# A recurrence with three chain banks on both diagonals of TensorE, and a triangular inverse in blocks of 16 that TensorE joins to blocks of 32

## The chip, the cores and the metric

The kernel runs on one core of one Trainium2 chip. Its time is the device time of one execution in microseconds (us). Three runs of the kernel before took 1589.51, 1591.01 and 1592.47 us; the median is 1591.01 us. The engines are named PE (TensorE's matmuls), PEld (its weight loads), DVE (VectorE), ACT (ScalarE), POOL (GpSimd) and SP (the engine that issues most DMAs).

## The reference

Two blocks over 512 tokens of width 1024 and 256 context tokens. The change lies in the first block's mixer, in its recurrent half: 8 heads of width 64, two directions, 768 steps each.

```
def wkv_scan(state0, r, decay, kk, b, v, k, reverse):
    def step(S, inp):
        r_t, w_t, kk_t, b_t, v_t, k_t = inp
        sa = jnp.einsum("bhvk,bhk->bhv", S, kk_t)
        S = (S * w_t[:, :, None, :] - sa[..., None] * b_t[:, :, None, :]
             + v_t[..., None] * k_t[:, :, None, :])
        return S, jnp.einsum("bhvk,bhk->bhv", S, r_t)
    ...
for d in range(N_DIR):
    decay = exp(-DECAY_SCALE * sigmoid(w0[d] + tanh(w_lo) @ w_up[d]))
    a = sigmoid(a0[d] + a_lo @ a_up[d])
    k_d = k * (1 + (a - 1) * k_a)
    state, y = wkv_scan(init[d], rh, to_heads(decay), kk, kk * to_heads(a), vh, to_heads(k_d),
                        reverse=(d == 1))
    y_sum = y if y_sum is None else y_sum + y
```

After it come a group norm and a gate of y, the projection `w_out`, a conv FFN, and the second block (gated recurrence, windowed attention, conv FFN). All of it is float32.

## The kernel before, in words

**The stages.** `proj` computes the first block's projections and, among them, the preparation of head pair 0. `rwkv` then runs four `stage(j)`, one for each pair of heads. A pair's two heads lie in the partitions 0–63 and 64–127, so one product of 64x64 is two matmuls (`mmh`, L633), one on each of two diagonal quadrants of the 128x128 array; in the trace each of them leaves two records. `tail` holds the rest, from `out_proj1` (L885) on.

**The chain.** The 768 tokens are 12 chunks of 64. A stage makes 12 steps g, each for both directions d: 48 steps in all. For a chunk, `pr` = AS·V + KR·S0 is copied to R (ACT, L757), `pu` = XT·R is copied to U (L759), `p3` = kbt·V + id·S0 + kbt·U becomes the next state S0 (L769), and `py` = AS·V + KR·S0 + AS·U becomes Y (L188). All four outputs of a direction lie in one PSUM bank (`c10`, `c11`), and a token (`order="c1{d}"`) keeps a bank's matmuls in the order in which the code writes them. AS is the masked product of `psc`, put in place by DVE (L731); `kbt` is evacuated by ACT.

**The inverse.** XT holds, for each chunk and direction, the inverse of a unit triangle of 64. `inverse` (L650) takes AK (from `prep`), transposes 32x32 blocks into U (L663), makes 31 row steps on DVE, each a multiplication (L671) and a subtraction (L672), transposes X to F1 and F2 (L674, L675), and joins blocks of 32 to 64 by TensorE with 32x32 matmuls (`pt` L691, `po` L698 and L699). Each pass over PSUM goes by halves `D` of 12 blocks; ACT evacuates them.

**The order.** A scheduler issues by priority. Each chain step hands out some units of `todo`, a chain of generators: `prep(j+1)` (low-rank products, decay, KB, KR, AK, then its `inverse`), after the last one `splits`, `ada12` and `first`. `ada12` loads 32 pieces of 512 KB on SP's queue and DVE reduces each (L538, L539); `first` splits `wout` for the first two output tiles of `out_proj1` (`ahead`), which `rwkv` multiplies after the chain. `ada12` starts once `prep(3)` is done and its pool is closed. Then `gn` of the last stage (L781) gives the last operand `ahi7`, and `px` is completed.

Of the kernel before, what the change touches and what calls it, by code (L numbers as in the profile page):

```python
# [18 lines left out]
P = 128  # L19
# [20 lines left out]
for _n, _w in (("ident", 128), ("ones", 128), ("blk", 128), ("hind", 2), ("m0", 192), ("m1", 192), ("id2", 64), ("bsel", 6), ("hsel", 128), ("scan", 780)):  # L40
    CST[_n] = (_off, _w)
    _off += _w
# [3 lines left out]
def lay(I):  # L46
# [30 lines left out]
    for n, (s, w) in VEC.items():  # L77
# [21 lines left out]
         "bsel": np.kron(np.eye(64, 6), np.ones((2, 1))), "hsel": np.concatenate([np.tile(np.kron(np.eye(2), np.ones((1, 64))), (6, 1)), np.zeros((116, P))], 0)}  # L99
    c["id2"] = np.concatenate([np.eye(64)] * 2, 0)  # L100
# [22 lines left out]
class K:  # L123
# [120 lines left out]
    def build(self):  # L244
        tc = self.tc
        with ExitStack() as es:
# [10 lines left out]
            with ExitStack() as er:  # L257
                r0 = self.r0 = self.pool(er, "r0", side="left")
                self.sg = r0.tile([P, NX], F32, name="sg")
                self.vD = self.dr.tile([P, 4, 12, 64], F32, name="vD")  # L260
                self.rD, self.kD, self.kkD = [[self.dr.tile([P, n], F32, name=f"{t}D{j}") for j in range(4)] for t, n in (("r", NX), ("k", NT), ("kk", NT))]
                st = lambda p, name, shape: p.tile([P] + shape, F32, name=name)
                XT0, XT1 = self.XT0, _ = st(r0, "XT0", [24, 64]), zxb[:, 5:8, :].rearrange("p a (b c) -> p (a b) c", c=64)
                set0 = {"KB": [st(r0, f"KB0{d}", [12, 2, 64]) for d in range(2)], "KR": [st(r0, f"KR0{d}", [1280]) for d in range(2)]}
                self.sets = [dict(set0, XT=XT0), {"XT": XT1}, None, dict(set0, XT=XT0)]
                self.hb, self.kah = st(r0, "hb", [16]), st(r0, "kah", [4, 4])
                with ExitStack() as ep:
                    self.pp = self.pool(ep, "pp", side="right")
# [8 lines left out]
                    self.AK = st(self.pp, "AK", [32, 64])  # L277
# [21 lines left out]
    def proj(self):  # L299
# [62 lines left out]
        nc.gpsimd.memset(self.AK, 0.0)  # L362

# [23 lines left out]
        def k_post(j, px, pc):  # L387
# [4 lines left out]
            kr = self.pp.tile([P, 1024], F32, tag="inv", name="kr", bufs=3)[:, 0:NT]  # L392
# [85 lines left out]
    def rwkv(self, es, ep):  # L478
# [5 lines left out]
        self.C1 = [self.ps2.tile([P, 512], F32, name=f"c1{d}") for d in range(2)]  # L484
        for t in (*self.AS[0], *self.AS[1]):
            nc.vector.memset(t, 0.0)
        todo, gn = self.todo, iter(())
        for j in range(4):
# [3 lines left out]
            if j == 1:  # L492
# [4 lines left out]
                self.mmbufs, self.axbufs, self.wbufs, self.wsbufs = 6, 2, 3, 4  # L497
# [46 lines left out]
    def prep(self, j):  # L544
# [26 lines left out]
        for d in range(2):  # L571
# [51 lines left out]
            for q in range(2):  # L623
                pa = psm(384, "pa")
                for c in range(6 * q, 6 * q + 6):
                    kp = krc[:, c, :] if c < 4 else krx[:, c - 4, 0, :]
                    lt, rt_ = (kp, kb[:, c, bs, :]) if d else (kb[:, c, bs, :], kp)
                    self.mmh(pa[:, (c - 6 * q) * 64:(c - 6 * q) * 64 + 64], lt, rt_)
# [21 lines left out]
    def inverse(self, j):  # L650
# [4 lines left out]
        big = lambda name: pp.tile([P, 32, 32], F32, tag="inv", name=name, bufs=3)  # L655
# [6 lines left out]
        U, tmp, X = big("U"), big("tmp").rearrange("p a b -> p (a b)"), big("X")  # L662
        nc.vector.transpose(out=U, in_=AK[:, :, 0:32].rearrange("p n i -> p i n"))  # L663
        nc.gpsimd.memset(X, 0.0)
        nc.gpsimd.memset(X.rearrange("p a b -> p (a b)")[:, ::33], 1.0)
        for k in range(31):
            if k % 4 == 0:
                yield
            n, w = 31 - k, k + 1
            tv = tmp[:, 0:n * w].rearrange("p (a b) -> p a b", b=w)  # L670
            nc.vector.tensor_tensor(out=tv, in0=U[:, k + 1:32, k:k + 1].to_broadcast([P, n, w]), in1=X[:, k:k + 1, 0:w].to_broadcast([P, n, w]), op=ALU.mult)  # L671
            nc.vector.tensor_tensor(out=X[:, k + 1:32, 0:w], in0=X[:, k + 1:32, 0:w], in1=tv, op=ALU.subtract)  # L672
# [4 lines left out]
        D = slice(0, 12), slice(12, 24)  # L677
        for r, F in zip(D, (F1, F2)):
# [5 lines left out]
        T = big("T")  # L684
        ps = lambda name: self.psp.tile([P, 12, 32], F32, tag="inv", name=name, bufs=1)
# [18 lines left out]
    def stage(self, j, S, todo, rb, gn):  # L704
# [35 lines left out]
        for g in range(12):  # L740
            at = base + self.PK * g
            with self.prio(at):
# [3 lines left out]
                for d in range(2):  # L746
# [7 lines left out]
                    mm(pr, A[:, 0:64], V, True, g == 0)  # L754
                    if g:
                        mm(pr, KR[:, 0:64], S0, False, True)
                    nc.scalar.activation(out=R, in_=pr, func=AF.Copy)  # L757
                    mm(pu, XT[:, 12 * d + c, :], R)
                    nc.scalar.activation(out=U, in_=pu, func=AF.Copy, scale=-1.0)  # L759
                    if g < 11:  # L760
                        mm(p3, kt[:, 0], V, True, False)
                        if g:
                            mm(p3, id2, S0, False, False)
                        mm(p3, kt[:, 1], U, False, True)
                    if x:
# [15 lines left out]
    def gn(self, j, Y, bo, vt):  # L781
# [46 lines left out]
        for i in range(8):  # L828
            self.mmh(py[:, i, :], yc[:, i, :], self.c("id2"))
# [9 lines left out]
    def tail(self):  # L839
        nc, A = self.nc, self.A  # L840
        with ExitStack() as es:
# [3 lines left out]
            self.xr = self.zx  # L845
            self.ps = self.psum(self.e3, "ps3", side="right")
# [38 lines left out]
    def out_proj1(self):  # L885
# [9 lines left out]
        for n in range(2, KD):  # L895
# [9 lines left out]
        for hf in range(2):  # L905
            c = slice(H * hf, H * hf + H)
            acc = None
            for n in range(KD):
                if n < 2:
# [7 lines left out]
                self.mm3(pm, [(*ws[n - 2](k), self.ahi[k][:, c], self.alo[k][:, c]) for k in range(KD)])  # L917
# [72 lines left out]
    def out_proj2(self, act, es, e6):  # L990
# [3 lines left out]
        for n in range(KD):  # L994
# [6 lines left out]
            if n == 1:  # L1001
                e6.close()
                self.ps = self.psum(es, "ps7")
                self.mmbufs = 6
# [392 lines left out]
```

## Time and profile before

| | |
|---|---|
| median of three runs | 1591.01 us |
| the profiled execution, its span | 1591.34 us, 1589.5 us |
| `proj` | up to about 256 us |
| the 48 chain steps | 266.0 to 517.4 us |
| PE, DVE, ACT busy over the whole span | 94%, 63%, 40% |

The profiled execution lies 0.33 us above the median; 1.84 us of it lie outside its span. A busy share of PE counts a matmul from its start to its modelled end; matmuls overlap, so in the chain, where a record of about 220 ns starts every 30 ns or so at best, 90% busy is not a full engine. Idle times carry the engine and line that ended them ("<-").

### The profile page before, as it was taken

To read this page: it belongs to the slowest core of one execution; us is meant where nothing else is said; L and a number is where in the kernel's file an instruction comes from. 1 tells how busy PE (TensorE), PEld (TensorE's weight loads), DVE (VectorE), ACT (ScalarE), POOL (GpSimd) and SP (SyncE) were. 2 spreads that over 40 slices of the span, in tenths; PEclk is the share of its full clock that TensorE was granted. 3 is DMA by queue.
4 is the path that set the end of the run, shared out by engine and by line. 5 is a ranking of instruction groups with operands and counts; after the bars stand their busy time and mean duration, and the time that the engine had idled before them with its cause. 6 is when DMAs were issued, how large, how long until landed. Compare 5 with 4: busy or idle time off the path is not lost. (4 is left out here: it accounts for less than half of the span.)

```text
span 1589.5 us, 28932 instructions
## 1 busy us (share of the span) xinstructions
PE 1498.6 (94%) x12062; PEld 1228.9 (77%) x12062; DVE 999.9 (63%) x1691; ACT 632.7 (40%) x1258; POOL 121.7 (8%) x141
## 2 busy tenths in 40 slices
PE   4899999989888999999999997999999999999998
PEld 2777787877777898888888875887677888888886
DVE  3436765777867669888863448588965555554221
ACT  3524343555453334333332325335554333333122
POOL 1111001020110000000000004121200000000000
PEclk9999898989999999999999998999999999999999
DMA  9243321010057613223323322211112222233221
GB/s 339 87 156 104 100 89 60 4 45 5 15 197 258 214 40 119 94 93 101 98 83 100 96 93 70 80 54 54 36 59 93 93 93 93 93 94 106 93 92 54
DMA packets 62179, 152.83 MB, mean 96 GB/s; under 512 B 12640, under 2 KB 14432, under 8 KB 62048
## 3 DMA queue, kind: packets, MB, share of 16 engines
q1 hardware_dynamic: 58016, 143.95, 27.9%
q10 hardware_dynamic: 4032, 7.04, 1.3%
q8 instruction: 94, 1.54, 0.4%
q14 instruction: 37, 0.30, 0.1%
HBM read 143.10 MB, written 7.86 MB: 95 GB/s over the span
## 5 line engine op out<-in xcount | busy, mean ns | idle before, releaser
L181 ACT ACTIVATE whi<-w 128x1024 fp32r<-128x1024 f32 (+2 forms) x220 | 208.7, 950 | 448.2 <-PE pm L170 333.3
L182 DVE TENSOR_TENSOR wlo<-w,whi 128x1024 fp32r<-128x1024 f32 (+2 forms) x212 | 229.9, 1086 | 201.3 <-ACT whi L181 195.3
L169 PE MATMUL pm<-ahi,whi 128*128 128x512 f32 (+1 forms) x624 | 236.4, 379 | 3.0 <-DVE sh L1080 2.6
L170 PE MATMUL pm<-alo,whi 128*128 128x512 f32 (+1 forms) x624 | 234.8, 376 | 0.0
L171 PE MATMUL pm<-ahi,wlo 128*128 128x512 f32 (+1 forms) x624 | 234.0, 375 | 0.0
L170 PE MATMUL pm<-al,whi 128*128 128x512 f32 x352 | 139.7, 397 | 0.0
L169 PE MATMUL pm<-ah,whi 128*128 128x512 f32 x352 | 139.2, 395 | 0.0
L171 PE MATMUL pm<-ah,wlo 128*128 128x512 f32 x352 | 139.2, 395 | 0.0
L169 PEld LDWEIGHTS pm<-ahi,whi 128*128 128x128 f32 x624 | 117.6, 189 | 24.2 <-ACT sh L1095 3.0
L171 PEld LDWEIGHTS pm<-ahi,wlo 128*128 128x128 f32 x624 | 117.6, 188 | 20.6 <-issue 0.7
L170 PEld LDWEIGHTS pm<-alo,whi 128*128 128x128 f32 x624 | 117.7, 189 | 20.3 <-issue 0.7
L953 DVE SCALAR_TENSOR_TENSOR cv<-pm,vec,cv 128x441 f32<-128x441 f32 (+2 forms) x176 | 121.1, 693 | 4.1
L170 PEld LDWEIGHTS pm<-al,whi 128*128 128x128 f32 x352 | 66.2, 188 | 16.1 <-issue 0.2
L171 PEld LDWEIGHTS pm<-ah,wlo 128*128 128x128 f32 x352 | 66.2, 188 | 16.1 <-issue 0.2
L169 PEld LDWEIGHTS pm<-ah,whi 128*128 128x128 f32 x352 | 66.2, 188 | 16.0
L171 PE MATMUL pm<-hhi,wlo 128*128 128x512 f32 x176 | 70.8, 402 | 2.7 <-DVE wlo L182 2.7
L169 PE MATMUL pm<-hhi,whi 128*128 128x512 f32 x176 | 71.4, 406 | 0.2 <-ACT whi L181 0.2
L170 PE MATMUL pm<-hlo,whi 128*128 128x512 f32 x176 | 70.6, 401 | 0.0
L169 PE MATMUL pd<-whi,gh 128*128 128x512 f32 x176 | 69.5, 395 | 0.0
L169 PE MATMUL pm<-hh,whi 128*128 128x512 f32 x176 | 69.3, 394 | 0.0
L170 PE MATMUL pm<-hl,whi 128*128 128x512 f32 x176 | 69.3, 394 | 0.0
L171 PE MATMUL pm<-hh,wlo 128*128 128x512 f32 x176 | 69.3, 394 | 0.0
(397 smaller groups left out, 3073.6 us busy)
## 6 DMA issues: line engine op xcount, KB each, us to landing
w<-in_fup SPq DMA_DIRECT2D x44, 512.0 KB, 3.7
adaw<-in_adat SPq DMA_DIRECT2D x32, 512.0 KB, 4.6
w<-in_win SPq DMA_DIRECT2D x44, 256.0 KB, 2.9
w<-in_wg SPq DMA_DIRECT2D x22, 512.0 KB, 3.6
w<-in_wu SPq DMA_DIRECT2D x22, 512.0 KB, 3.6
w<-in_wd SPq DMA_DIRECT2D x22, 512.0 KB, 3.7
w<-in_win SPq DMA_DIRECT2D x18, 512.0 KB, 3.5
w<-in_wout SPq DMA_DIRECT2D x16, 512.0 KB, 3.8
```

What stands on the lines that cost most here:

```text
L169: nc.tensor.matmul(out, lh, rh, start=(first and i == 0), stop=False)
L170: nc.tensor.matmul(out, lh, rl, start=False, stop=False)
L171: nc.tensor.matmul(out, ll, rh, start=False, stop=(last and i == n - 1))
L181: self.nc.scalar.activation(out=hi, in_=src, func=AF.Copy)
L182: (eng or self.nc.vector).tensor_tensor(out=lo, in0=src, in1=hi.bitcast(F32), op=ALU.subtract)
L953: nc.vector.scalar_tensor_tensor(out=o, in0=p[:, ro[0] + dr:ro[1] + dr, co[0] + dc:co[1] + dc], scalar=w(i), in1=o, op0=ALU.mult, op1=ALU.add)
```

## The change

It has four parts.

1. `mmh` gets `swap`: the matmuls of `pr`, `pu`, `py`, of `pa` in `prep` and of `py` in `gn` write to the other half of the partitions, and so run on the two quadrants off the diagonal. `p3`, `psc`, `pkt` and `pv` stay on the diagonal.
2. `p3` moves from the banks `c10` and `c11` to a third bank `c2`, which both directions share with an order token of its own. Its V and S0 terms stand ahead of `pu` in the code.
3. `inverse` makes 15 row steps on two triangles of 16 at once. A new tile AM holds the block between them (DVE, `copy_predicated`). Six passes `every` of 48 matmuls of 32x32 join the triangles: two are evacuated by ACT to T, four are subtracted by DVE from F1 and F2.
4. Space in PSUM: `pt` and `po` share one buffer with `prep`'s `pb`, `pl` and `pa`; `ahead` holds one output tile of `out_proj1` instead of two, and the second is computed with the others.

```
-    def mmh(self, out, lt, rt, start=True, stop=True, order=None):
+    def mmh(self, out, lt, rt, start=True, stop=True, order=None, swap=False):
         for h in range(2):
-            hs = slice(64 * h, 64 * h + 64)
-            m = self.nc.tensor.matmul(out[hs], lt[hs], rt[hs], start=start, stop=stop)
+            hs, ho = (slice(64 * i, 64 * i + 64) for i in (h, h ^ swap))
+            m = self.nc.tensor.matmul(out[ho], lt[hs], rt[hs], start=start, stop=stop)
...
-        for k in range(31):
+        for k in range(15):
             if k % 4 == 0:
                 yield
-            n, w = 31 - k, k + 1
...
+            n, w = 15 - k, k + 1
+            tv = tmp[:, 0:2 * n * w].rearrange("p (h a b) -> p h a b", h=2, b=w)
+            nc.vector.tensor_tensor(out=tv, in0=U2[:, :, k + 1:16, k:k + 1].to_broadcast([P, 2, n, w]), in1=X2[:, :, k:k + 1, 0:w].to_broadcast([P, 2, n, w]), op=ALU.mult)
+            nc.vector.tensor_tensor(out=X2[:, :, k + 1:16, 0:w], in0=X2[:, :, k + 1:16, 0:w], in1=tv, op=ALU.subtract)
...
+        ps = lambda name: self.psp.tile([P, 12, 32], F32, tag="mm", name=name, bufs=1)
+        def every(out, r, lt, rt):
+            for n in range(r.start, r.stop):
+                for o in range(0, P, 32):
+                    nc.tensor.matmul(out[o:o + 32, n - r.start, :], lt[o:o + 32, n, :], rt[o:o + 32, n, :], start=True, stop=True)
+        for r in D:
+            yield
+            pt = ps("pt")
+            every(pt, r, self.AM, F2)
+            self.copy(nc.scalar, T[:, r, :], pt)
+        for r in D:
+            yield
+            pt = ps("pt")
+            every(pt, r, F1, T)
+            nc.vector.tensor_tensor(out=F2[:, r, :], in0=F2[:, r, :], in1=pt, op=ALU.subtract)
+            yield
+            pt = ps("pt")
+            every(pt, r, T, F1)
+            nc.vector.tensor_tensor(out=F1[:, r, :], in0=F1[:, r, :], in1=pt, op=ALU.subtract)
...
-        ps = lambda name: self.psp.tile([P, 12, 32], F32, tag="inv", name=name, bufs=1)
...
-                    pr, pu, py, p3 = (self.C1[d][:, i * 64:i * 64 + 64] for i in range(4))
-                    mm = lambda *a: self.mmh(*a, order=f"c1{d}")
+                    pr, pu, py = (self.C1[d][:, i * 64:i * 64 + 64] for i in range(3))
+                    p3 = self.C2[:, d * 64:d * 64 + 64]
+                    m1 = lambda *a: self.mmh(*a, order=f"c1{d}", swap=True)
+                    m2 = lambda *a: self.mmh(*a, order="c2")
...
                     nc.scalar.activation(out=R, in_=pr, func=AF.Copy)
-                    mm(pu, XT[:, 12 * d + c, :], R)
+                    if g < 11:
+                        m2(p3, kt[:, 0], V, True, False)
+                        if g:
+                            m2(p3, id2, S0, False, False)
+                    m1(pu, XT[:, 12 * d + c, :], R)
                     nc.scalar.activation(out=U, in_=pu, func=AF.Copy, scale=-1.0)
...
-        for n in range(2):
-            self.ahead.append((self.psax(), self.wsplit(self.A["wout"][n], KD, P)))
+        for n in range(1):
+            self.ahead.append((self.psa.tile([P, NX], F32, name="ah"), self.wsplit(self.A["wout"][n], KD, P)))
```

The first place is PE in a step of the chain in the last stage. `c10` and `c11` are the banks of the two directions, RU is R or U, `cst` the identity, and `py` the group norm's.

```order
2105 L638 MATMUL c11_2378<-RU11_2374,AS12_2370 64x64 x2
2106 L638 MATMUL pkt_5894<-cst_60,KB01_85 64x64 x5
2107 L638 MATMUL c10_2377<-vt_5497,AS00_2365 64x64 x2
2108 L638 MATMUL c10_2377<-S00_2375,KR00_86 64x64 x2
2109 L638 MATMUL py_5958<-cst_60,yc_5686 64x64 x5
2110 L638 MATMUL c10_2377<-RU00_2371,XT0_83 64x64 x2
2111 L638 MATMUL py_5958<-cst_60,yc_5686 64x64 x4
2112 L638 MATMUL c11_2378<-vt_5497,AS10_2368 64x64
2113 L638 MATMUL c10_2377<-vt_5497,kbt_5891 64x64 x2
2114 L638 MATMUL c10_2377<-S00_2375,cst_60 64x64 x2
2115 L638 MATMUL c10_2377<-RU00_2371,kbt_5891 64x64 x2
```

And the changed kernel at the like place, where `c2` is the shared bank:

```order
2110 L641 MATMUL c10_2649<-RU01_2644,XT0_83 64x64 x2
2111 L641 MATMUL py_7037<-cst_60,yc_6765 64x64 x2
2112 L641 MATMUL c2_2651<-vt_6576,kbt_6970 64x64 x2
2113 L641 MATMUL c2_2651<-S00_2647,cst_60 64x64 x2
2114 L641 MATMUL c10_2649<-vt_6576,AS00_2637 64x64 x2
2115 L641 MATMUL c10_2649<-S00_2647,KR00_86 64x64 x2
2116 L641 MATMUL c2_2651<-RU01_2644,kbt_6970 64x64 x2
2117 L641 MATMUL c10_2649<-RU01_2644,AS00_2637 64x64 x2
2118 L641 MATMUL c11_2650<-vt_6576,AS10_2640 64x64 x2
2119 L641 MATMUL c11_2650<-S01_2648,KR01_87 64x64 x2
```

The terms of `p3` and `py` that don't need U now stand ahead of the first matmul that does, and after it only two matmuls are left of each.

The second place is PE in the inverse of pair 2, in the changed kernel: the six joins are the rows of `pt` by 48, and what stands between them is chain steps of stage 1 (`c10`, `c11`, `c2`, `psc`, `pkt`).

```order
1398 L694 MATMUL pt_4067<-T_3822,F1_3818 32x32 x48
1399 L641 MATMUL c2_2651<-S00_2647,cst_60 64x64
1400 L641 MATMUL c10_2649<-vt_4396,AS00_2637 64x64 x2
1401 L641 MATMUL c10_2649<-S00_2647,KR10_1919 64x64 x2
1402 L641 MATMUL c2_2651<-RU01_2644,kbt_4728 64x64 x2
1403 L641 MATMUL c10_2649<-RU01_2644,AS02_2639 64x64 x2
1404 L641 MATMUL c11_2650<-vt_4396,AS12_2642 64x64 x2
1405 L641 MATMUL c11_2650<-S01_2648,KR11_1920 64x64
1406 L694 MATMUL pt_4203<-F1_3818,T_3822 32x32 x48
```

In the kernel before nothing stands there; its inverse has only the rows of `pt` from AK and `po`, which follow in both. Between two joins stand six or seven products of the chain, and each join waits for the evacuation of the one ahead of it, since `pt` has one buffer.

The third place is ACT at the end of the recurrence, in the changed kernel: `whi` are splits of `wout`, R and U of the last two steps stand among them.

```order
653 L189 ACTIVATE kbt_7269<-pkt_7251 128x256
654 L182 ACTIVATE whi_7435<-w_7433 128x1024
655 L189 ACTIVATE kbt_7290<-pkt_7272 128x256
656 L792 ACTIVATE RU00_2643<-c10_2649 128x64
657 L182 ACTIVATE whi_7551<-w_7549 128x1024
658 L798 ACTIVATE RU00_2643<-c10_2649 128x64
659 L792 ACTIVATE RU10_2645<-c11_2650 128x64
660 L182 ACTIVATE whi_7557<-w_7555 128x1024
661 L804 ACTIVATE S00_2647<-c2_2651,pc_4557 128x64
662 L189 ACTIVATE Y_6578<-c10_2649 128x64
```

Before, the chain's last copy stands ahead of all four splits:

```order
658 L757 ACTIVATE RU11_2374<-c11_2378 128x64
659 L759 ACTIVATE RU11_2374<-c11_2378 128x64
660 L188 ACTIVATE Y_5500<-c11_2378 128x64
661 L181 ACTIVATE whi_6356<-w_6354 128x1024
662 L794 ACTIVATE zx_65<-pv_6368,vec_61 128x512
663 L181 ACTIVATE whi_6363<-w_6361 128x1024
```

The splits have moved ahead of the chain's last two steps; their `w` comes by a DMA that SP issues behind the last piece of `ada12`.

## Rows read from the trace of the kernel before

**Rows 1.** The page: the span.
```profile
span 1589.5 us, 28932 instructions
```

**Rows 2.** Windows: stretch; its length, busy PE, PEld, DVE, ACT, POOL; clock, DMA.
```profile
300.00:360.00 60.00, 53.33 (x1224) 45.11 (x1218) 43.85 (x87) 33.67 (x107) 10.55 (x16) 0.89 0.10 31
```

**Rows 3.** Line L757: count; ns min/median/max, first and last start.
```profile
L757 ACT ACTIVATE RU<-c x96: 210/219/234, 266.0 to 515.8; 128x64 f32<-128x64 f32 x96
```

**Rows 4.** ACT, 300.5 to 306 us: start, duration, engine, line, operation [idle before].
```profile
301.06 0.31 ACT L769 ACTIVATE S<-c,pc 128x64 f32<-128x64 f32 x1 [0.96 <-PE c L638]
301.28 0.38 ACT L188 ACTIVATE kbt<-pkt 128x256 f32<-128x256 f32 x1
...
302.20 0.22 ACT L759 ACTIVATE RU<-c 128x64 f32<-128x64 f32 x1 [0.16 <-PE c L638]
303.38 0.31 ACT L769 ACTIVATE S<-c,pc 128x64 f32<-128x64 f32 x1 [0.96 <-PE c L638]
...
305.42 0.31 ACT L769 ACTIVATE S<-c,pc 128x64 f32<-128x64 f32 x1 [0.96 <-PE c L638]
```

**Rows 5.** PE in the same stretch.
```profile
301.82 0.33 PE L638 MATMUL c<-RU,XT 64*64 64x64 f32 x4
...
302.75 0.28 PE L638 MATMUL c<-RU,kbt 64*64 64x64 f32 x4
302.87 0.28 PE L638 MATMUL c<-vt,AS 64*64 64x64 f32 x4
```

**Rows 6.** Groups of lines, DVE, 398.4 to 434.5 us, busy, mean ns | idle before.
```profile
L672 DVE TENSOR_TENSOR X<-X,tmp 128x31 f32<-128x31 f32 (+15 forms) x31 | 11.6, 373 | 0.8
L671 DVE TENSOR_TENSOR tmp<-U,X 128x31 f32<-128x31 f32 (+15 forms) x31 | 11.0, 355 | 1.0
L731 DVE COPY_PREDICATED AS<-cst,psc 128x384 f32<-128x384 int32 (+1 forms) x6 | 3.0, 492 | 2.0 <-PE psc L638 2.0
```

**Rows 7.** DVE in order of time, at three places of two inverses.
```profile
175.77 0.38 DVE L671 TENSOR_TENSOR tmp<-U,X 128x207 f32<-128x207 f32 x1
...
181.90 0.19 DVE L671 TENSOR_TENSOR tmp<-U,X 128x31 f32<-128x31 f32 x1
...
434.55 1.96 DVE L674 STREAM_TRANSPOSE F<-X 128x1024 f32<-128x1024 f32 x1
```

**Rows 8.** The joins of before: their matmuls (L698, L699, L691) and evacuations.
```profile
L698 PE MATMUL po<-F,T x48: 191/191/212, 313.1 to 313.9; 32*32 32x32 f32 x48
...
L699 PE MATMUL po<-T,F x48: 191/191/212, 313.1 to 313.9; 32*32 32x32 f32 x48
...
439.89 0.48 ACT L188 ACTIVATE T<-pt 32x384 f32<-32x384 f32 x1
...
443.51 1.96 ACT L188 ACTIVATE XT<-po 32x384 f32<-32x384 f32 x4 [0.75 <-PE po L699]
...
186.18 1.21 PE L691 MATMUL pt<-F,AK 32*32 32x32 f32 x48 [2.19 <-DVE F L675]
```

**Rows 9.** The end of the recurrence, on DVE, ACT and PE.
```profile
515.55 1.22 DVE L539 SCALAR_TENSOR_TENSOR adaw<-adaw,cb 128x1024 f32<-128x1024 f32 x1 [0.68 <-DMA adaw<-in_adat]
...
517.36 0.22 ACT L188 ACTIVATE Y<-c 128x64 f32<-128x64 f32 x1 [0.67 <-PE c L638]
517.98 1.06 ACT L181 ACTIVATE whi<-w 128x1024 fp32r<-128x1024 f32 x1 [0.40 <-DMA w<-in_wout]
...
524.48 1.06 ACT L181 ACTIVATE whi<-w 128x1024 fp32r<-128x1024 f32 x1 [1.09 <-DMA w<-in_wout]
...
534.08 0.75 DVE L830 SCALAR_TENSOR_TENSOR zx<-py,vec,zx 128x512 f32<-128x512 f32 x1 [5.44 <-PE py L638]
...
532.33 0.39 PE L170 MATMUL px<-alo,whi 128*128 128x512 f32 x1
532.56 0.39 PE L171 MATMUL px<-ahi,wlo 128*128 128x512 f32 x1
...
536.27 0.73 PE L169 MATMUL px<-ahi,whi 128*128 128x512 f32 x2 [1.35 <-ACT ahi L181]
```

More of the change, by code (lines that the diff above doesn't have):

```diff
@@ L39 @@
 _off = 0
-for _n, _w in (("ident", 128), ("ones", 128), ("blk", 128), ("hind", 2), ("m0", 192), ("m1", 192), ("id2", 64), ("bsel", 6), ("hsel", 128), ("scan", 780)):
+for _n, _w in (("ident", 128), ("ones", 128), ("blk", 128), ("hind", 2), ("m0", 192), ("m1", 192), ("id2", 64), ("m16", 32), ("bsel", 6), ("hsel", 128), ("scan", 780)):
     CST[_n] = (_off, _w)
@@ L276, in build @@
                     self.psp = self.psum(ep, "psp", side="right")
-                    self.AK = st(self.pp, "AK", [32, 64])
+                    self.AK, self.AM = st(self.pp, "AK", [32, 64]), st(self.pp, "AM", [24, 32])
                     with ExitStack() as e1:
@@ L362, in proj @@
         nc.gpsimd.memset(self.AK, 0.0)
+        nc.gpsimd.memset(self.AM, 0.0)
         def tile_of(u, x=True, c=True):
@@ L391, in k_post @@
             nc.sync.dma_start(out=self.kD[j], in_=kt)
-            kr = self.pp.tile([P, 1024], F32, tag="inv", name="kr", bufs=3)[:, 0:NT]
+            kr = self.pp.tile([P, 1056], F32, tag="inv", name="kr", bufs=3)[:, 0:NT]
             nc.vector.tensor_scalar(out=kr, in0=kt, scalar1=self.v("kk", j), scalar2=None, op0=ALU.mult)
@@ L484, in rwkv @@
         self.C1 = [self.ps2.tile([P, 512], F32, name=f"c1{d}") for d in range(2)]
+        self.C2 = self.ps2.tile([P, 512], F32, name="c2")
         for t in (*self.AS[0], *self.AS[1]):
@@ L654, in inverse @@
         nc, pp = self.nc, self.pp
-        big = lambda name: pp.tile([P, 32, 32], F32, tag="inv", name=name, bufs=3)
+        raw = lambda name: pp.tile([P, 1056], F32, tag="inv", name=name, bufs=3)
+        full = lambda t: t[:, 0:1024].rearrange("p (a b) -> p a b", b=32)
+        big = lambda name: full(raw(name))
+        two = lambda t: t.rearrange("p (h x) -> p h x", h=2)[:, :, 0:512].rearrange("p h (a b) -> p h a b", b=32)
         XT, AK = self.S[j]["XT"], self.AK
@@ L661, in inverse @@
         yield
-        U, tmp, X = big("U"), big("tmp").rearrange("p a b -> p (a b)"), big("X")
-        nc.vector.transpose(out=U, in_=AK[:, :, 0:32].rearrange("p n i -> p i n"))
+        U, tmp, X = raw("U"), raw("tmp"), raw("X")
+        nc.vector.transpose(out=full(U), in_=AK[:, :, 0:32].rearrange("p n i -> p i n"))
+        nc.vector.copy_predicated(self.AM, self.c("m16").bitcast(I32).unsqueeze(1).to_broadcast([P, 24, 32]), AK[:, 0:24, 0:32])
         nc.gpsimd.memset(X, 0.0)
-        nc.gpsimd.memset(X.rearrange("p a b -> p (a b)")[:, ::33], 1.0)
-        for k in range(31):
+        nc.gpsimd.memset(X[:, 0:1024:33], 1.0)
+        U2, X2 = two(U), two(X)
+        for k in range(15):
             if k % 4 == 0:
                 yield
-            n, w = 31 - k, k + 1
-            tv = tmp[:, 0:n * w].rearrange("p (a b) -> p a b", b=w)
-            nc.vector.tensor_tensor(out=tv, in0=U[:, k + 1:32, k:k + 1].to_broadcast([P, n, w]), in1=X[:, k:k + 1, 0:w].to_broadcast([P, n, w]), op=ALU.mult)
-            nc.vector.tensor_tensor(out=X[:, k + 1:32, 0:w], in0=X[:, k + 1:32, 0:w], in1=tv, op=ALU.subtract)
+            n, w = 15 - k, k + 1
+            tv = tmp[:, 0:2 * n * w].rearrange("p (h a b) -> p h a b", h=2, b=w)
+            nc.vector.tensor_tensor(out=tv, in0=U2[:, :, k + 1:16, k:k + 1].to_broadcast([P, 2, n, w]), in1=X2[:, :, k:k + 1, 0:w].to_broadcast([P, 2, n, w]), op=ALU.mult)
+            nc.vector.tensor_tensor(out=X2[:, :, k + 1:16, 0:w], in0=X2[:, :, k + 1:16, 0:w], in1=tv, op=ALU.subtract)
+        X = full(X)
         F1, F2 = big("F1"), big("F2")
@@ L677, in inverse @@
         D = slice(0, 12), slice(12, 24)
+        ps = lambda name: self.psp.tile([P, 12, 32], F32, tag="mm", name=name, bufs=1)
+        T = big("T")
+        def every(out, r, lt, rt):
[16 more added lines that the diff above has]
+            nc.vector.tensor_tensor(out=F1[:, r, :], in0=F1[:, r, :], in1=pt, op=ALU.subtract)
+        yield
         for r, F in zip(D, (F1, F2)):
@@ L682, in inverse @@
             nc.gpsimd.memset(XT[b0[h], D[1], 32:64], 0.0)
-        T = big("T")
-        ps = lambda name: self.psp.tile([P, 12, 32], F32, tag="inv", name=name, bufs=1)
         for r in D:
@@ L845, in tail @@
             self.xr = self.zx
+            self.psa = None
             self.ps = self.psum(self.e3, "ps3", side="right")
@@ L894, in out_proj1 @@
         ws = []
-        for n in range(2, KD):
+        for n in range(1, KD):
             if n < self.WO:
@@ L908, in out_proj1 @@
             for n in range(KD):
-                if n < 2:
+                if n < 1:
                     if hf == 0:
@@ L916, in out_proj1 @@
                 pm = self.psmm(H)
-                self.mm3(pm, [(*ws[n - 2](k), self.ahi[k][:, c], self.alo[k][:, c]) for k in range(KD)])
+                self.mm3(pm, [(*ws[n - 1](k), self.ahi[k][:, c], self.alo[k][:, c]) for k in range(KD)])
                 nc.vector.scalar_tensor_tensor(out=self.xr[n][:, c], in0=pm, scalar=g1[:, n:n + 1], in1=xin[n][:, c], op0=ALU.mult, op1=ALU.add)
@@ L1003, in out_proj2 @@
                 self.ps = self.psum(es, "ps7")
-                self.mmbufs = 6
+                self.mmbufs, self.axbufs = 6, 2
         bc, _ = self.rsqrt_bc(acc, NX, 1.0 / 1024, 1e-6, self.q)
```

25 lines of the change are left out of this document (11 added, 14 removed).

## The prediction

> **What bounds the kernel now.** I read the page first. The span is 1589.5 us [rows 1]; the median of the runs, 1591.01 us, is 0.33 us under the profiled execution, so the sum below, made on that execution (1591.34 us), may stand for the median. The work that the change touches is the recurrence: the chain's first copy starts at 266.0 us [rows 3], its last at 517.36 [rows 9], 251 us for 48 steps, 5.24 each.
>
> Next I read the windows: in 300 to 360 us DVE is busy 43.85 of 60 us and ACT 33.67 [rows 2]. PE's 53.33 is a sum over overlapping matmuls. No engine is full, so waiting in order sets the pace. Then I read ACT and PE in order of time where only the chain moves. The S copies of the two directions come at 301.06, 303.38 and 305.42 [rows 4]: 4.36 us for a whole step, and before each ACT stands idle 0.96 us for a matmul of the chain. The two directions do not overlap there: PE issues the products of one direction in a row, 0.12 us apart [rows 5], behind one bank's order.
>
> The rest of a step's mean is interference. Up to the end of the last preparation the chain makes 33 steps (by the order of instructions; `prep(3)` ends with XT at 443.51 + 1.96, the first of its four copies at about 443.5 [rows 8]): (443.5 − 266.0)/33 = 5.38 us a step, 1.02 above 4.36, so about 12 us for twelve steps, the length of one preparation. After that `ada12` starts, and from there its 32 loads, not the chain, set the end: DVE's last reduction, at 515.55, waits 0.68 us on its DMA [rows 9], and the chain's last copy follows at 517.36. So the first question is when `prep(3)` ends, the second what stands behind the last load.
>
> **The chain.** A direction's own loop after the change is: `pr`·S0 0.33 (one product, as `pu` [rows 5]), R 0.22, `pu` 0.33, U 0.22, `p3`·U 0.33, S 0.31 [rows 3 to 5], or 1.74 us, with six hand-overs. A hand-over of the like is seen from `pu` (301.82 + 0.33) to U (302.20): 0.05. That makes 2.05. The two directions can now overlap, since PE has issued V's and S0's terms of `p3` and `py` before U comes; they share only `c2` and ACT. ACT needs for a step with output 2 × (0.31 + 3 × 0.22) and 0.38 of `kbt` twice every other step, so 2.3 us, up to 2.7 where both fall in one. The bounds are thus 2.3 us, where the loop and ACT run full, and 4.36, where nothing overlaps. In between I take 3.2: PE still takes both directions' products in one queue, and ACT's copies come in one order, so a late one holds the other direction. Running on both diagonals I cost at nothing beside this: a step's products at 0.12 each are not what it waits for.
>
> **The inverse.** On DVE, 62 row operations cost 22.6 us in 36.1 us of stretch [rows 6]. One costs 0.19 us at 31 elements and 0.38 at 207 [rows 7], so 0.0011 us an element and 0.16 at none. After the change there are 30, with twice the sum of n·w for k up to 14, 1360 elements in all over the 15 pairs: 2 × (15 × 0.16 + 1360 × 0.0011) = 7.8 us. AM's masked copy of 768 elements is two of AS's of at most 384 (0.49 on the mean [rows 6]), 1.0; four subtractions of 384 from PSUM at about the same 0.5 make 2.0. DVE thus falls by 22.6 − 10.8 = 11.8 us an inverse.
>
> On PE, six joins of 48 matmuls are added. Such a matmul leaves two records; 96 records over four positions of the array go from 313.1 to 313.9 us, 0.8 us [rows 8], about 8 ns each, so six joins are 4.6 to 5 us. Each join waits for the one ahead: 0.8 of issue, 0.19 of the last, the evacuation 0.48 (ACT) or 0.5 (DVE), hand-overs 0.1 to 0.2, about 1.7 us. Between two of them PE has six or seven products of the chain at 0.12, 0.8 us. So PE stands 0.9 us at most beyond its work if the evacuating engine is free. Six times (0.9 and about 0.4 of the join's own issue that covers no waiting) I take as 8 us for a preparation. Lowest is nothing, where the chain's waits cover it. Highest is 3 us a join, 18 us, where the evacuation stands behind an instruction that itself waits (DVE's waits for `psc`: 2.0 us in this stretch alone [rows 6]). I take 8, nearer to the rows without queueing.
>
> Against the trace stands a rule: the matmuls of L698 and L699 start 8 ns apart [rows 8]. The Trainium skill (TensorE: Matmul & The Clock Gate, "Wait — 56ns, not 53.3ns?") says that start to start never falls under about 25 ns, however few the columns. By that, taken for each matmul, an inverse's 576 records would cost 14.4 us instead of 4.6, some 10 us more in each of four inverses, and the sum below would come out near 1615; the trace does not bear that out for matmuls at four positions, so I give it no chance of its own.
>
> DVE's relief of 11.8 us pays only where DVE holds PE. I leave the interference at 12 us for twelve steps, and add the joins' 8: the relief I count as paying for AM, for the loss of overlap (`pt` now shares `prep`'s only buffer, so the next preparation starts after the joins) and for the wait of the 768-element copy. Twelve steps then cost 12 × 3.2 + 12 + 8 = 58.4 us against 64.6, or 4.87 a step.
>
> In `proj` the inverse of pair 0 gives DVE the same 11.8 us, and takes away at most the 2.19 us that PE waited for F [rows 8]; it adds 5 us of PE and six waits with only three big matmuls between. Bounds −2 and +6; I take +1, between the ends and under the 2.4 us by which the matmuls exceed the wait, since the wait may also go with some of the waits of the joins.
>
> **The end.** In the changed order `prep(3)` is done after 31 steps, not 33. The chain starts at 267, so T = 267 + 31 × 4.87 = 418, 25.5 us earlier than 443.5. I leave the pace of `ada12` as it is, bound by its loads. Its last reduction comes 25.5 earlier. Behind it the change loses: R and U of the last two steps stand behind four splits of `wout` on ACT. The first and last split start 2.4 and 8.9 us after the last reduction, the last ends at 525.54 [rows 9]; then R, `pu`, U, a product of `py` and Y, 0.22 + 0.33 + 0.22 + 0.33 + 0.22 and hand-overs, 1.6, with the other direction's some 2.2. The chain's end is thus 12.2 us behind the last reduction instead of 1.8 (with Y's start, 517.36). From that copy to `px` with `ahi7` it took 536.27 − 517.36 = 18.9 us, of which the group norm's `py` stood 5.44 us behind `px`'s first 42 matmuls [rows 9]. Those go, so 13.5. The second tile's 24 matmuls, 0.23 apart, come later, 5.5 us. The end is then 12.2 + 13.5 + 5.5 = 31.2 after the last reduction, against 20.7 before: +10.5.
>
> The sum: −25.5 + 10.5 = −15.0, or 1591.3 − 15.0 = 1576.3; predicted 1576.
>
> **The rivals.** (1) Joins in a queue. The mechanism sits in `inverse`: a join's evacuation stands behind waiting work on ACT or DVE, PE stands meanwhile, and the chain with it, as the shared buffer lets nothing else of `prep` run. At 3 us a join, 18 for a preparation, and with a step of 3.2: 68.4 for twelve, 5.7 a step, T = 444, no earlier; plus 10.5 gives 1602, slower. It decides from 2.4 us a join on, where T is 433. Against it: DVE is freed of 11.8 us in the same stretch. For it: PE has one queue, and a step of the chain has few products to fill 1.7 us.
>
> (2) The inverse was the path. From 398.4 to 434.5 us the row steps filled 22.6 us of 36.1 on DVE, and F1's transpose follows the last of them at once [rows 6, 7]. If preparations are bound by their own sequence, and the row steps now run nearly unhindered (7.8 + 1.0 for 34 us before the transposes) with joins of 1.3 us, 8 an inverse, each preparation is 17 us shorter, T = 443.5 − 52 = 392, and the time 1591.3 − 52 + 10.5 = 1550. Against it: the chain would have to make 31 steps in 125 us, 4.0 each with all interference. The Trainium skill (TensorEngine Tiling (Array Packing), "PSUM Bottleneck") warns that tiling speeds up TensorE but not the copies from PSUM; the ACT copies of the rows above are unchanged, and by them 2.3 us a step remain, which would leave 1.7 for interference.
>
> (3) The chain does not overlap. If the shared `c2` and ACT's order leave a step at 4.36 − 0.5 and joins cost 8 for twelve: 3.86 × 12 + 20 = 66.3, 5.53 a step, T = 438; −5.1 + 10.5 = +5.4, 1597. With a little less interference it is no change: T = 433, 1591.
>
> **How the numbers follow.** Forecast, 1564 to 1588: 0.44. Rival 2, below: 0.22. Rival 3: 0.12, half of it within 0.2%. Rival 1: 0.18. 0.04 is left for a lower clock or a loss in the tail that I don't see. A measurement here can tell a difference of about 0.2%, 3.2 us. Faster is the forecast and rival 2: 0.66. The same: 0.08. Slower: 0.26. The range reaches down to 1546 for rival 2 and up to 1604 for rival 1; the forecast's own is 1564 to 1588.
>
> **What will show it.** The S copies of one direction 3.2 us apart where no join runs, and the two directions overlapped; X's row steps near 7.8 us an inverse; joins 1.7 us apart; the first reduction of `ada12` some 25 us earlier; 12 us from the last reduction to the chain's last copy. A first reduction no earlier than 445 us makes the forecast wrong, as does a step of 4 us or more without joins, or `ada12` paced other than before.

## The result, and the profile after

The changed kernel takes 1628.53 us (median of four runs, 1625.57 to 1633.18), against 1590.26 us for the kernel before, measured together with it (median of four): a ratio of 1.0245, 95% interval 1.022 to 1.027. It is slower by 38 us; forecast were 15 us faster, with a range up to 1604. The profiled execution took 1628.61 us.

The page of the changed kernel, span, engines and the queue that carries instructions (its row reads "q8 instruction: 94, 1.54, 0.4%" before):

```profile
span 1626.8 us, 33489 instructions
PE 1514.0 (93%) x14390; PEld 1239.9 (76%) x14390; DVE 962.7 (59%) x1584; ACT 633.0 (39%) x1268; POOL 125.4 (8%) x142
...
q8 instruction: 113, 1.85, 0.5%
```

PE has 2328 records more, and as many weight loads; 2304 of each are the joins' (four inverses with 576). The instruction queue moved 19 packets more; 0.31 MB over 19 is 16 KB each.

R's first and last start in the changed kernel, and the reductions of `ada12` (against 266.0 to 515.8 [rows 3] and 515.55 for the last reduction [rows 9]):

```profile
L792 ACT ACTIVATE RU<-c x96: 205/220/242, 275.7 to 562.0; 128x64 f32<-128x64 f32 x96
...
L542 DVE SCALAR_TENSOR_TENSOR adaw<-adaw,cb x32: 1202/1224/2104, 487.7 to 551.9; 128x1024 f32<-128x1024 f32 x32
```

And the four copies of XT that end `prep(3)` (443.51 before [rows 8]):

```profile
478.39 1.96 ACT L189 ACTIVATE XT<-po 32x384 f32<-32x384 f32 x4 [1.28 <-PE po L731]
```

The chain starts 9.7 us late, and the last reduction comes 36.4 us late. The 32 reductions start over 64.2 us, about as before (451.9 to 515.6, 63.7 us): `ada12` keeps its pace, and what is late is the end of `prep(3)`, by 34.9 us.

The S copies of one stage in the changed kernel, on ACT, in order of time:

```profile
277.42 0.31 ACT L804 ACTIVATE S<-c,pc 128x64 f32<-128x64 f32 x1 [0.25 <-PE c L641]
278.52 0.31 ACT L804 ACTIVATE S<-c,pc 128x64 f32<-128x64 f32 x1 [0.52 <-PE c L641]
280.52 0.31 ACT L804 ACTIVATE S<-c,pc 128x64 f32<-128x64 f32 x1 [0.52 <-PE c L641]
281.90 0.31 ACT L804 ACTIVATE S<-c,pc 128x64 f32<-128x64 f32 x1 [0.95 <-PE c L641]
283.90 0.31 ACT L804 ACTIVATE S<-c,pc 128x64 f32<-128x64 f32 x1 [0.52 <-PE c L641]
...
292.06 0.31 ACT L804 ACTIVATE S<-c,pc 128x64 f32<-128x64 f32 x1
...
304.68 0.31 ACT L804 ACTIVATE S<-c,pc 128x64 f32<-128x64 f32 x1 [2.97 <-PE c L641]
...
322.73 0.31 ACT L804 ACTIVATE S<-c,pc 128x64 f32<-128x64 f32 x1 [0.25 <-PE c L641]
```

Without joins a direction's copies are 3.1 and 3.4 us apart, near the forecast's step of 3.2 (4.36 in [rows 4]). Then two steps take 30.7 us, from 292.06 to 322.73. Five of the six joins, the old joins and the start of the next preparation lie there. The windows of these stretches (time, length, PE busy with its records, granted clock, DMA), the last of them from 150 us to the end of the chain:

```profile
276.00:288.00 12.00, 11.41 (x219) 0.50 0.01 1
294.00:296.00 2.00, 0.71 (x19) 0.72 0.00 0
290.00:300.00 10.00, 7.75 (x414) 0.74 0.02 6
300.00:310.00 10.00, 8.59 (x334) 0.50 0.02 3
310.00:320.00 10.00, 9.80 (x279) 0.50 0.02 3
320.00:330.00 10.00, 9.87 (x160) 0.55 0.01 3
150.00:565.00 415.00, 357.07 (x8428) 0.84 0.27 84
```

The same view of the kernel before:

```profile
266.00:278.00 12.00, 12.00 (x133) 0.50 0.01 1
300.00:306.00 6.00, 5.97 (x150) 1.00 0.03 7
150.00:520.00 370.00, 335.88 (x6144) 0.93 0.28 89
```

Two of the joins of the third preparation in the changed kernel, PE in order of time:

```profile
453.15 0.64 PE L694 MATMUL pt<-F,AM 32*32 32x32 f32 x51
455.01 0.59 PE L694 MATMUL pt<-F,AM 32*32 32x32 f32 x45 [1.22 <-issue]
...
456.35 0.75 PE L694 MATMUL pt<-T,F 32*32 32x32 f32 x65
459.01 0.65 PE L694 MATMUL pt<-T,F 32*32 32x32 f32 x31 [1.91 <-issue]
```

A join breaks off in the middle, with no semaphore to wait for: PE stands 1.22 and 1.91 us, put down to issue, which means that the profile shows nothing that it waits for. The windows from the end of one stop to the end of the next (time, length, then PE and its weight loads PEld with their counts, DVE, ACT, POOL, clock, DMA):

```profile
455.00:459.00 4.00, 2.10 (x128) 1.89 (x128) 0.58 (x1) 0.49 (x1) 0.00 (x0) 0.96 0.01 4
459.00:462.45 3.45, 2.64 (x128) 2.38 (x128) 0.56 (x1) 0.50 (x2) 0.00 (x0) 0.50 0.02 5
```

From stop to stop PE makes 128 matmul records, those of the chain among them, and 128 weight loads: 256 instructions. Over the stretch with the recurrence and the inverse ahead of it the waits of PE add up so (in total, times, longest):

```profile
PE pt L694 <- issue: 13.7, 13, 1.9
PE c L641 <- DVE AS L763: 9.7, 9, 3.2
```

All of PE's stops put down to issue come to 16.6 us there, against 0.6 before; the wait for AS was 5.9 before. From about 295 to 328 us, some 33 us, the granted clock is 0.50, that is 1.2 GHz, where the kernel before shows 1.00 in 300 to 320 us; it fell in 294 to 296 us, where PE was busy for 0.71 of 2 us. The lower level by itself is not new: it stands ahead of the joins too (276 to 288 us), and before the change in 266 to 278 us. New is its share: the mean is 0.84, against 0.93 before. So two things are new that my sum did not have: PE stops in the joins, and it is at the lower level for longer.

### The profile page after: what moved, and what is told of

It is laid out like the page before. It is cut to its first block, busy times and chain, and to the rows that moved or that the text cites. A ratio compares the mean times of both kernels' runs of the same rounds, so it can differ in the third digit from the quotient of the medians.

```text
span 1626.8 us, 33489 instructions
## 1 busy us (share of the span) xinstructions
PE 1514.0 (93%) x14390; PEld 1239.9 (76%) x14390; DVE 962.7 (59%) x1584; ACT 633.0 (39%) x1268; POOL 125.4 (8%) x142
## 5 line engine op out<-in xcount | busy, mean ns | idle before, releaser
L182 ACT ACTIVATE whi<-w 128x1024 fp32r<-128x1024 f32 (+2 forms) x220 | 209.0, 951 | 451.0 <-PE pm L171 335.6
L170 PE MATMUL pm<-ahi,whi 128*128 128x512 f32 (+1 forms) x640 | 241.6, 378 | 0.4 <-DVE zx L1032 0.4
L171 PE MATMUL pm<-alo,whi 128*128 128x512 f32 (+1 forms) x640 | 239.6, 374 | 0.0
L172 PE MATMUL pm<-ahi,wlo 128*128 128x512 f32 (+1 forms) x640 | 238.7, 373 | 0.0
L170 PEld LDWEIGHTS pm<-ahi,whi 128*128 128x128 f32 x640 | 120.9, 189 | 21.3 <-issue 0.8
L172 PEld LDWEIGHTS pm<-ahi,wlo 128*128 128x128 f32 x640 | 120.9, 189 | 20.9 <-issue 0.7
L171 PEld LDWEIGHTS pm<-alo,whi 128*128 128x128 f32 x640 | 121.0, 189 | 20.4 <-issue 0.9
L641 PE MATMUL c<-vt,AS 64*64 64x64 f32 x640 | 61.0, 264 | 13.9 <-DVE AS L763 9.7
L172 PE MATMUL pd<-whi,gl 128*128 128x512 f32 x176 | 69.5, 395 | 0.0
L171 PE MATMUL pd<-wlo,gh 128*128 128x512 f32 x176 | 69.5, 395 | 0.0
```

The lines of the kernel that those rows point to most:

```text
L170: nc.tensor.matmul(out, lh, rh, start=(first and i == 0), stop=False)
L171: nc.tensor.matmul(out, lh, rl, start=False, stop=False)
L172: nc.tensor.matmul(out, ll, rh, start=False, stop=(last and i == n - 1))
L182: self.nc.scalar.activation(out=hi, in_=src, func=AF.Copy)
L641: m = self.nc.tensor.matmul(out[ho], lt[hs], rt[hs], start=start, stop=stop)
```

## The experiments

Times are medians. Each ratio is to runs of the kernel before measured together with the version, with its 95% interval; it is worked out from all runs, and so can differ by some tenths of a per cent from the ratio of two medians.

**a_chain: the old inverse in the changed kernel.** The 31 row steps are back; swapped quadrants, `c2` and the shared buffer stay.

```
-        for k in range(15):
+        for k in range(31):
...
-            every(pt, r, self.AM, F2)
```

> The changed kernel with the old inverse: 31 row steps on DVE, no joins of 16 to 32; the swapped quadrants, the bank c2 and the buffer shared by the inverse and prep stay. Theory A (the joins are the loss, the chain is a gain): stages lose the stretch of about 30 us at half clock, the chain keeps its 3.2 us steps, and the time falls under the kernel before, to 1560 to 1580 us. Rival B (the shared bank c2 and the shared buffer are the loss, the joins are innocent): the time stays near 1628. Rival C (the chain's own change gives nothing, the joins cost all): about 1591.

1591.16 us, ratio 1.0009 (0.9991 to 1.0028): C's number. But its reason falls with the trace: the chain is faster (steps of 3.1 to 3.4 us, last copy 4.9 us earlier than before), while the loads of `ada12` start at 451.0 instead of 441.8 us, since `prep(3)` ends later. B falls: the 37 us lie in the new inverse.

**b_inv: the new inverse in the kernel before,** with a PSUM buffer of its own.

> The kernel before with the new inverse alone: 15 row steps and six joins, in a PSUM buffer of its own; chain, banks and order as before. Theory A: the joins cost some 20 us in each of the three inverses of the recurrence, the chain gives nothing back: 1630 to 1650 us, with the clock at half after each inverse. Rival B: faster than before, 1570 to 1590, since DVE has 11 us less in each inverse and the buffer is not shared. Rival C: about 1628, as the changed kernel.

1617.20 us, ratio 1.0164 (1.014 to 1.0189), under A's range and over B's. The inverse alone makes the kernel 26 us slower, with DVE's relief and without a shared buffer; stops by issue are 10.0 us in the joins and 17.4 us in all. The mean granted clock from 150 us to the end of the chain (556) is 0.92, against 0.93 before: this loss is hardly one of the clock.

**c_warm: a large matmul ahead of each join.**

```
         def every(out, r, lt, rt):
+            nc.tensor.matmul(out, self.c("ident"), F1[:, r, :], start=True, stop=True)
```

> The changed kernel with one more matmul of 128x128 by 384 columns ahead of each join, into the tile that the join then overwrites (24 matmuls added in all). Theory A1 (the half clock after the joins is what costs, and it falls because matmuls of 32x32 leave the array nearly empty): the clock in the joins' stretch rises over 0.5, and the time falls by 5 to 25 us, though 24 matmuls are added. Rival A2 (the joins' own waits and the stops in PE's instruction stream cost, the clock follows them): the clock stays at 0.5 there and the time rises by 0 to 10 us.

1627.23 us, ratio 1.0231 (1.0215 to 1.0248): no change against the changed kernel. The medians of the joins' matmuls fell from 236 to 191 ns in four of the six, so they now ran at the higher level (the mean from 150 to 560 us is 0.90, against 0.84), and the stops fell from 16.6 to 10.4 us in all; but each added matmul has two records that hold PE 0.9 us, 22 us in 24. Neither theory's picture fits. It leaves open how much of the loss is the lower clock by itself.

**d_half: half the matmuls in each join, of 64 columns.**

```
-            for n in range(r.start, r.stop):
+            for n in range(r.start, r.stop, 2):
                 for o in range(0, P, 32):
-                    nc.tensor.matmul(out[o:o + 32, n - r.start, :], lt[o:o + 32, n, :], rt[o:o + 32, n, :], start=True, stop=True)
+                    nc.tensor.matmul(out[o:o + 32, n - r.start:n + 2 - r.start, :], lt[o:o + 32, n, :], rt[o:o + 32, n:n + 2, :], start=True, stop=True)
```

> The changed kernel with half the matmuls in each join, each of 64 columns instead of 32: the second of two blocks is multiplied by the weights of the first, so what the inverse computes is not the inverse. Columns, evacuations and waits stay, instructions of the joins are halved. Theory A2a (PE's instruction stream runs dry in the joins): the stops put down to issue in pt fall from 13.7 us to under 5, and the time falls by 10 us or more. Rival A2b (the chain of six joins with their evacuations costs, whatever the number of instructions): the time moves by less than 5 us.

1591.82 us, ratio 1.0019 (1.0004 to 1.0035): 36.7 us come back. Its joins on PE:

```profile
282.26 0.87 PE L694 MATMUL pt<-F,AM 32*32 32x64 f32 x48
283.75 0.87 PE L694 MATMUL pt<-T,F 32*32 32x64 f32 x48
285.58 0.98 PE L694 MATMUL pt<-F,T 32*32 32x64 f32 x48
287.68 0.87 PE L694 MATMUL pt<-T,F 32*32 32x64 f32 x48
289.23 1.26 PE L694 MATMUL pt<-F,T 32*32 32x64 f32 x48
```

Most joins still take 0.87 us, against 1.02 for 96 records at the full clock in the changed kernel, so the array's own time hardly fell. No join breaks off any more, joins follow each other every 1.5 to 2.1 us (2.9 to 3.3 on the mean of an inverse before the edit), the granted clock is 1.00 from 280 to 300 us, and the chain starts at 266.0 us instead of 275.7. What the edit removed is instructions, matmuls and weight loads; the two changes of tile size at each join stayed, so these are not the loss.

**e_loose: the joins' matmuls without their chain,** added to the kernel before.

```
+            pt = ps("pl")
+            for i in range(3):
+                for n in range(r.start, r.stop):
+                    for o in range(0, P, 32):
+                        nc.tensor.matmul(pt[o:o + 32, n - r.start, :], F1[o:o + 32, n, :], F2[o:o + 32, n, :], start=True, stop=True)
+                yield
```

> The kernel before with 288 matmuls of 32x32 more in each inverse, in six passes of 48 over the four positions, into a tile that nobody uses (ACT reads one column of it after each three passes, to free it). No chain of joins, all 31 row steps kept. Theory A2a (the number of PE instructions in a burst is the price): stops by issue of 8 to 14 us, and 15 to 30 us slower than before, about as much as the new inverse in the kernel before (+26). Theory A2b (the chain of joins is the price): only the matmuls' own 5 us in each of four inverses where nothing hides them, at most +10, with few stops.

1643.29 us, ratio 1.0340 (1.0321 to 1.0359): 54 us, more than A2a's range, with 24.7 us of stops. Theory A2b falls. One inverse, PE in order of time:

```profile
315.59 2.50 PE L692 MATMUL pl<-F,F 32*32 32x32 f32 x247 [0.93 <-DVE F L675]
320.27 0.56 PE L692 MATMUL pl<-F,F 32*32 32x32 f32 x41 [2.18 <-issue]
...
323.39 1.47 PE L692 MATMUL pl<-F,F 32*32 32x32 f32 x129
327.32 1.93 PE L692 MATMUL pl<-F,F 32*32 32x32 f32 x128 [2.46 <-issue]
331.32 0.65 PE L692 MATMUL pl<-F,F 32*32 32x32 f32 x31 [2.07 <-issue]
```

Between two stops stand 128 matmul records (64 matmuls as the code writes them) with 128 weight loads: 256 instructions, as in the changed kernel, every 3.9 and 4.0 us, or 31 ns a record with its stop, though within a run of them they start 8 to 15 ns apart. The Trainium skill (Runtime: NRT & Kernel Launch, "Instruction fetch mechanics") says that an engine's instructions come in blocks of 16 KiB, 256 instructions, which the trace bears out by the 256 and by the packets of 16 KB; that the cost of a block is mostly hidden, as the same section says, does not hold here, where a stop is 2.07 to 2.46 us. That PE waits in these stops for its next block is thus concluded from the count; no row of the profile names it.

**f_one: one matmul a join.** What it computes is not the inverse.

```
-            for n in range(r.start, r.stop):
-                for o in range(0, P, 32):
-                    nc.tensor.matmul(out[o:o + 32, n - r.start, :], ...
+            nc.tensor.matmul(out, lt[:, r.start:r.start + 4, :], rt[:, r, :], start=True, stop=True)
```

> The changed kernel with one matmul of 128x128 by 384 columns in place of the 48 of each join: what it computes is not the inverse; the six joins, their evacuations, their buffer and their waits stay. Theory A2a (instructions): the joins' stretch shrinks further than in the run with half of the matmuls, to 1565 to 1580 us. Theory A2b (round trips): it stays within 5 us of that run's 1591.8.

1589.23 us, ratio 1.0000 (0.9983 to 1.0017): A2b's number. With half the matmuls the price of instructions was already gone; what is left of the loss against the forecast's 1576 is something else.

**j_onebank: f_one with a PSUM buffer of its own for the inverse,** and three buffers for psc and the like.

```
-        ps = lambda name: self.psp.tile([P, 12, 32], F32, tag="mm", name=name, bufs=1)
+        ps = lambda name: self.psp.tile([P, 12, 32], F32, tag="inv", name=name, bufs=1)
```

> The changed kernel with one matmul of 128x128 by 384 columns in place of the 48 of each join (not the inverse any more), and with a PSUM buffer of its own for the inverse, at the price of one of the four buffers of psc, pkt, pv, pg and py. It asks where DVE's relief went once the instructions are gone. Theory P (the shared buffer kept the next preparation waiting, as with the old inverse, where a buffer of its own gave 10.6 us): 1570 to 1580 us. Rival Q (the six joins in a row, each with its evacuation, take what DVE gave): within 5 us of 1589.2.

1571.59 us, ratio 0.9897 (0.9849 to 0.9945): Theory P. `ada12`'s loads start at 409.6 us instead of 432.7. With the buffer apart the time is 17.6 us under f_one's, though psc and the like lost one.

**g_bank: the same buffers, with the old inverse.**

> The changed kernel with the old inverse, and with a PSUM buffer for it apart from prep's, at the price of one of the four buffers of psc, pkt, pv, pg and py. Theory: with the shared buffer the next preparation waited for the end of the inverse, so prep(3)'s end came 9 us later (the loads of ada12 at 451.0 instead of 441.8 us) though the steps were faster; with a buffer of its own the loads start at 425 to 440 and the time is 1570 to 1582. Rival: three buffers hold the chain back as much, 1588 to 1595.

1580.59 us, ratio 0.9940 (0.9919 to 0.9960). This version computes all of the reference and is faster than both kernels; against the changed one by 48 us. The loads start at 437.4.

**i_two: g_bank with two output tiles ahead.**

```
-        for n in range(1):
-            self.ahead.append((self.psa.tile([P, NX], F32, name="ah"), self.wsplit(self.A["wout"][n], KD, P)))
+        for n in range(2):
+            self.ahead.append((self.psax(), self.wsplit(self.A["wout"][n], KD, P)))
```

> The run with the old inverse, a buffer of its own for it, three chain banks and both diagonals, and also two output tiles of out_proj1 ahead, as before the change. If the second tile's 24 matmuls find waiting time of PE behind the chain, 1574 to 1579 us, some 3 to 5 us under the run with one tile; if wout's second piece comes too late behind ada12's loads, no change, 1580.

1583.16 us, ratio 0.9952 (0.9934 to 0.9970). The intervals overlap: no gain. The tile that the change gave up cost nothing that shows here.

**n_noswap: a_chain with all of swap off.**

> The changed kernel with the old inverse and without the other diagonal: all of swap is off, the third bank c2 and the order of the chain stay. If the off-diagonal quadrants are what makes a step 3 to 3.5 us instead of 4.3, the steps go back to about 4 and the time rises by 3 to 10 us over 1591.2. If it is the bank and the order (V's and S0's terms ahead of U), steps and time stay within 3 us.

1598.46 us, ratio 1.0061 (1.0041 to 1.0081), 7.3 us over a_chain. Its first steps are 2.7 us, but at a granted clock of 1.00 (267.5 to 276.6 us), where those of a_chain, 3.1 to 3.4 us, stand at 0.50 (269 to 279 us). At 1.00 (271 to 277 us) and with swap, j_onebank has

```profile
269.92 0.31 ACT L802 ACTIVATE S<-c,pc 128x64 f32<-128x64 f32 x1 [0.17 <-PE c L641]
...
272.64 0.31 ACT L802 ACTIVATE S<-c,pc 128x64 f32<-128x64 f32 x1 [0.38 <-PE c L641]
...
275.29 0.31 ACT L802 ACTIVATE S<-c,pc 128x64 f32<-128x64 f32 x1 [0.38 <-PE c L641]
```

that is 2.7 us too. So the other diagonal is worth something (the loads start at 456.7 instead of 451.0), but these steps do not show where.

**h_spread: the loose matmuls spread over the chain.**

```
                     mm(pu, XT[:, 12 * d + c, :], R)
+                    for i in range(3):
+                        for o in range(0, P, 32):
+                            m = self.nc.tensor.matmul(self.C1[d][o:o + 32, 256 + 32 * i:288 + 32 * i], id2[o:o + 32, 0:32], V[o:o + 32, 0:32], start=True, stop=True)
```

> The kernel before with the same number of loose matmuls as the run with loose matmuls in the inverse (1152 of 32x32 in all), but spread: 12 in each of the 96 steps of a direction, ahead of p3, into columns of c10 and c11 that nobody reads. Theory S (a burst outruns the delivery of PE's instructions; what counts is records per us): a step then has about 108 records in 4.3 us, 25 per us, under the 32 per us at which the loose bursts were delivered, so few stops, and 1590 to 1605 us. Rival T (each instruction costs about 47 ns wherever it stands): about 1643, as with the bursts.

1625.75 us, ratio 1.0219 (1.0189 to 1.0248): S failed, and T with it. Stops are fewer (9.7 us against 24.7). PE around one such group:

```profile
302.88 0.28 PE L638 MATMUL c<-RU,XT 64*64 64x64 f32 x4
303.09 0.39 PE L761 MATMUL c<-vt,cst 32*32 32x32 f32 x24
303.41 0.33 PE L638 MATMUL c<-vt,AS 64*64 64x64 f32 x4
```

From XT to AS it is 0.53 us, where two products follow each other at 0.12 [rows 5]: the group costs 0.41 us, 0.19 of it at 8 ns a record, and I put the other 0.2 down to the two changes of tile size. 96 groups of it are 39 us on the chain, about the 35 to 37 measured (by the ratio and by the medians). My expectation also counted a step's records too low: in 300 to 306 us PE makes 184, 31 a us instead of 25. So the run does not separate delivery from this; that stays open.

## Why the prediction was wrong

**The chain: overlapped as forecast, its size met by luck.** The two directions overlap, and steps of 3.1 to 3.4 us stand against 3.2 taken. But they stand at a granted clock of 0.50, and the rows that the 3.2 was worked out from at 1.00; at 1.00 a step is 2.7 (j_onebank), still between the bounds of 2.3 and 4.36. The swap at nothing was wrong by some 7 us, and not in these steps.

**The row steps: right.** X's 45 pairs in three inverses take 13.1 + 13.1 us, 8.7 an inverse (7.8), the subtractions 0.554 us each (0.5), AM 1.11 (1.0).

**The joins: the step that failed.** I priced an inverse's 576 records at 8 ns each, 4.6 us, from 96 records in 0.8 us [rows 8], and the whole of the joins at 8 us a preparation with an end of 18. The 96 records were one burst, shorter than the 128 that stand between two stops. Six joins in a row with the chain's records between them run into the stops: at e_loose's 31 ns a record 576 would be 18 us (an estimate), and with the lower clock beside it two steps took 30.7 us. The length of a preparation shows the price: from the chain's first copy to the XT of `prep(3)` three of them take 202.7 us, 67.6 each, where my sum had 50.3 (from 267 to 418) and the kernel before has 59.2. With half of the joins' instructions it is 58.3 us, with one matmul a join 56.3, and with the buffer apart too 48.7. The first reduction of `ada12` starts at 487.7 us, past the 445 that I had named as a sign of being wrong. Halving the instructions alone gave back 36.7 us of the 38 lost, and adding the instructions without the joins' chain (e_loose) cost 54.

The rule of the Trainium skill that I set aside (TensorE: Matmul & The Clock Gate, "Wait — 56ns, not 53.3ns?"), with start to start of 25 ns at least, would have put the time at 1615, nearer than my 1576. It is not the mechanism: matmuls at four positions do start 8 ns apart between two stops. But I dropped its number without asking what a longer burst would do.

**The shared buffer: mis-sized.** I let DVE's relief pay for it. By g_bank and j_onebank it cost 10.6 and 17.6 us (with one buffer of psc given up in both).

**`proj`: wrong by the same cause.** +1 forecast, bounds −2 and +6; the chain starts 9.7 us late, and not at all late with half the instructions. Its inverse breaks off too (1.60 and 1.45 us in the second and third join).

**The end: two terms right, the third not there.** From the last reduction (551.90) to the chain's last copy at 564.2 it is 12.3 us (12.2), and from there to `ahi7`'s product 11.5 (13.5):

```profile
551.90 1.23 DVE L542 SCALAR_TENSOR_TENSOR adaw<-adaw,cb 128x1024 f32<-128x1024 f32 x1 [0.45 <-DMA adaw<-in_adat]
...
563.84 0.57 ACT L189 ACTIVATE Y<-c 128x64 f32<-128x64 f32 x2 [0.69 <-PE c L641]
...
575.68 0.50 PE L170 MATMUL ah<-ahi,whi 128*128 128x512 f32 x1 [0.71 <-ACT ahi L182]
```

The second tile's 5.5 us do not show. From `ahi7`'s product to the end of the span it is 1051.1 us, against 1053.2 before (536.27 [rows 9] to 1589.5), and i_two, which gets the tile back, is no faster. So the end as a whole, from the last reduction on, grew by 1.0 us (1074.9 against 1073.9), not by 10.5. These are single executions, but the versions with the same end (c_warm, d_half, f_one, j_onebank) agree: from the end of the chain's last copy to the end of the span they and the changed kernel take 1061.8 to 1065.1 us, the kernel before 1071.9, where my terms made no difference. With 1.0 in place of 10.5 the forecast would have been 1567, farther off. Why the tile costs nothing is open.

**The rivals.** Rival 1 named the place, the joins and PE standing in them, and decided from 2.4 us a join; the joins came 2.9 to 3.3 us apart on the mean. But they did so not behind a waiting evacuation (from 291 to 308 us each evacuation starts at most 0.11 us behind its join): PE stopped for 3 to 4.4 us in each of the three inverses, and at the lower level a join's 96 records take 1.50 us instead of 1.02. With the instructions and the buffer taken out the time is 1571.6 us against 1576. That is near in part by luck: j_onebank's joins are one matmul each, and its chain ends 19.5 us behind the last reduction, not 12.2.

How the 36.7 us divide between the stops and the lower clock is not settled. The stops do not need the lower clock to cost time: b_inv lost 26 us with its mean clock at 0.92, against 0.93 before.

## What to carry to other kernels

Count a change's instructions, not only its busy time: a burst of small matmuls ran at its own pace here only up to the next stop, and behind that at 128 records with their weight loads in some 4 us. With half as many matmuls of twice the columns the new inverse took no longer than the old one (d_half; that version prices the instructions, it does not compute the inverse). When a step comes out as forecast, look whether the clock is the one of the rows that it was worked out from. And before two stages are made to share a buffer, look for the work that overlaps there now.

## What the runs showed of the hardware that was not expected

In a burst of small matmuls PE stops without any semaphore, after every 128 matmul records with their weight loads: for 0.4 to 1.9 us in the joins of the changed kernel, for 2.07 to 2.46 us in e_loose. A group of 32x32 records between products of 64x64 cost 0.2 us more than its records at 8 ns (one group of h_spread). The granted clock fell to 0.50 in the joins and stayed there for some 33 us, though PE was busy 86 to 99% of each 10 us from 300 us on; it also fell without such joins, for some 12 us at the start of the chain before the change.
